# adaLN sums in a 2-layer trunk: a third row-block buffer, low parts in temporaries, sums amid the next pair, small rows through Pool's queue

## The chip, the cores and the metric

One core of a Trainium2 chip runs the whole program. The metric is the device time of one execution in microseconds. Its engines each take their own instructions in program order and wait for one another by semaphores: TensorE (PE) multiplies, VectorE (DVE), ScalarE (ACT) and GpSimd (Pool) work elementwise, and SyncE (SP) issues most of the DMAs; ACT and Pool can issue DMAs too.

## The reference

Two layers of three sublayers each on x of 512 tokens x 1024, all in float32:

```python
c_act = jax.nn.silu(c)
for l in range(DEPTH):
    mod = (c_act @ ada_w[l] + ada_b[l]).reshape(b, N_SUB, 3, 1, D_MODEL)
    h = modulate(x, mod[:, 0, 0], mod[:, 0, 1])
    y = swiglu_ffn(h, ffn1_w_in[l], ffn1_w_out[l])
    x = layer_norm(ALPHA * x + 0.5 * mod[:, 0, 2] * y, ln_g[l, 0], ln_b[l, 0])
    h = modulate(x, mod[:, 1, 0], mod[:, 1, 1])
    proj = h @ mix_w_in[l]
    ...
    x = layer_norm(ALPHA * x + mod[:, 1, 2] * y, ln_g[l, 1], ln_b[l, 1])
    ...
```

The third sublayer is an FFN like the first. The mixer between them is a Mamba-2 scan, an attention and a short convolution side by side. "adaLN" is the first line of the loop: from one vector c come, for each sublayer, a shift, a scale and a gate of 1024 numbers, through a 1024 x 9216 matrix for each layer.

## The kernel before

The sublayers are numbered s = 0 to 5; 1 and 4 are mixers, the others FFNs. A float32 product is made as three matmuls on parts (mm3): each weight block is loaded (ri, or ro for the second matrix; SP), ACT copies its high part (hi, ho) and DVE subtracts it to get the low part (li, lo); the activations are split likewise into hh and hl. So every block costs PE three matmuls for each row of 128, and PE does most of the work.

**An FFN** runs over 11 pairs of column blocks. A pair is two loads (gate and up matrix) of two blocks each, hence four units of 24 matmuls, pf_pair_which_j, in the order 0_0, 1_0, 0_1, 1_1, and then silu (sg), product (af) and split (ah, al). The first pair of an FFN runs in token halves of 256, since the last tile's normalization is still under way. The split weights lie in 6 buffers each, so a block's split waits for the unit six earlier. After pair 5 and after pair 10 out_proj multiplies by the second matrix (po).

**adaLN's matrix product** is not on PE: ada_acc loads eight row blocks (ra, 128x1024, two buffers) and DVE adds each, times a column of silu(c), into two accumulators of 512 (acc, k = 0 to 7; 16 operations). What remains is a sum over the 128 partitions: acc_split makes a high and a low part of each accumulator (gh on ACT, gl on DVE), acc_sum multiplies both by a matrix of ones on PE. For a gate the sum goes through pg into the gate; for shift and scale through pm, then DVE picks the diagonal (dg) and reduces (ada_ss, pieces `which` 1 and 0).

These pieces are Python generators in a list, and tick(), called twice in every pair, advances the first of them by a few steps, so that they are recorded amid an FFN's pairs. A scheduler then orders each engine's instructions by what it reckons; the order is fixed when the program is built. The row blocks of adaLN are named by their first column: gate of s = 0 is acc_2048, then acc_4096 and acc_3072 (scale and shift of the mixer), acc_5120, acc_7168, acc_6144.

**x_affine** multiplies x by the last layer norm's g and adds its b in place (x, after the transposes that feed the next product have read it): 16 Pool operations of 128x512 on four tiles x_102 to x_105. Its vectors lng and lnb are loaded by ln_vectors on ACT's queue. **Pool's rs** is a power of 128x1 in each tile's layer norm. Two sets of small rows (rows_v for vT, rows_ln for lnT), loaded in s = 0, become columns by PE transposes (pv_vT, pv_lnT) after pair 3.

**A mixer** begins with pv (hidden v and the twelve decay inputs of each token), then the B, C and x features (pjm1b, pjm1c, pjm1x: each a product with splits lm.. on DVE). From pv's twelve columns DVE computes a softplus in a chain of tiny operations on 128x48 (v, av, zz, z, ppl, dt, a), and PE sums a over tokens in pcs, which the program places inside pjm1b.

Of the kernel before, what the change touches and what calls it, by code (L numbers as in the profile page):

```python
# [15 lines left out]
P = 128  # L16
# [9 lines left out]
RMS_EPS = 1e-5  # L26
NEG = -1.0e30
NLONG = 28
NTMP = 9
NW = 6  # L30
PAD_W = 16
POS = 1
BPOS = 2
TICK = object()
CR = (2.7, 1.3)
WSZ = 1024

# [32 lines left out]
def trunk(ctx, tc, x, c, ln_in_g, ln_in_b, ada_w, ada_b, ffn1_w_in, ffn1_w_out,  # L70
# [11 lines left out]

    shift("pad0", PAD_W)
    rawp = ctx.enter_context(tc.tile_pool(name="rawp", bufs=2))
    adap = ctx.enter_context(tc.tile_pool(name="adap", bufs=2))
    whp = ctx.enter_context(tc.tile_pool(name="whp", bufs=NW))
    wlp = ctx.enter_context(tc.tile_pool(name="wlp", bufs=NW))
    lp = ctx.enter_context(tc.tile_pool(name="lp", bufs=NLONG))
# [47 lines left out]

    def rows_v(l):
        rows = slot([NROW, P], F32, f"rows{l}")
        act.dma_start(rows[0:72, :], ada_b[l].rearrange("(r p) -> r p", p=P))
        act.dma_start(rows[R_CW:R_CB, :], ssd_conv_w[l].rearrange("k (c p) -> (k c) p", p=P))  # L140
        act.dma_start(rows[R_CB:R_SW, :], ssd_conv_b[l].rearrange("(c p) -> c p", p=P))
        act.dma_start(rows[R_SW:R_NG, :], sconv_w[l].rearrange("k (c p) -> (k c) p", p=P))
        act.dma_start(rows[R_NG:NROW, :], ssd_norm_g[l].rearrange("(c p) -> c p", p=P))
        return rows

    def rows_ln():
        rows = slot([96, P], F32, "rowsl")
        act.dma_start(rows[0:48, :], ln_g.rearrange("l j (r p) -> (l j r) p", p=P))
        act.dma_start(rows[48:96, :], ln_b.rearrange("l j (r p) -> (l j r) p", p=P))
        return rows  # L150

    def rows_first():
# [93 lines left out]
    def acc_split(acc):  # L246

        parts = []
        los = adap.tile([P, 2, 512], F32R, tag="ra", name="gl")
        for h in range(2):  # L250
            hi, lo = tmp([P, 512], "gh", F32R), los[:, h]
            act.activation(hi, acc[h], AF.Copy)
            dve.tensor_tensor(lo, acc[h], hi.bitcast(F32), ALU.subtract)
            parts.append((hi, lo))
        return parts

    def acc_sum(ps, hi, lo):
# [26 lines left out]
    def ada_ss(s):  # L284
        l, j = divmod(s, 3)
        new_mod(s)
        pres = []
        for which in (1, 0):
            acc = None
            for a in ada_acc(l, (j * 3 + which) * D):  # L290
                acc = acc if a is TICK else a
                yield a
            sums = sm.tile([P, KD], F32, tag=f"sums{which}", name=f"sums{which}", bufs=1)
            parts = acc_split(acc)
            yield TICK
# [50 lines left out]
    def ada_gate(s):  # L346
        l, j = divmod(s, 3)
        col = (j * 3 + 2) * D
        gate = [slot([P, 512], F32, f"gate{s}_{h}") for h in range(2)]
        for h in range(2):  # L350
            sp.dma_start(gate[h], ada_b[l, col + h * 512:col + h * 512 + 512].partition_broadcast(P))
        acc = None
        for a in ada_acc(l, col):
            acc = acc if a is TICK else a
            yield a
        parts = acc_split(acc)
        yield TICK
        for h in range(2):
            ps = pb([P, 512], f"pg{s}_{h}")
            acc_sum(ps, *parts[h])  # L360
            dve.tensor_tensor(gate[h], ps, gate[h], ALU.add)
        gates[s] = gate

    def ln_vectors(s):
        g, b = (ln_in_g, ln_in_b) if s == 0 else (ln_g[(s - 1) // 3, (s - 1) % 3], ln_b[(s - 1) // 3, (s - 1) % 3])
        for n, v in (("g", g), ("b", b)):
            for h in range(2):
                a = slot([P, 512], F32, f"ln{n}{s}_{h}")
                act.dma_start(a, v[h * 512:(h + 1) * 512].partition_broadcast(P))
# [6 lines left out]
    def begin(*gens):  # L376
# [2 lines left out]
        credit[0] = 0.0  # L379
        credit[1] = len(pending) and CR[0] if len(gens) > 2 else CR[1]  # L380

    def tick():
        credit[0] += credit[1]
        while pending and credit[0] >= 1:
            try:
                if next(pending[0]) is TICK:
                    break
                credit[0] -= 1
            except StopIteration:
                pending.pop(0)  # L390

# [237 lines left out]
        last[0] = act_last[0]  # L629
        return banks, units[2]  # L630

    def x_affine(s, eng):

        ln_vectors(s)
        for t in range(NT):
            for h in range(2):
                xh = xt[t][:, h * 512:(h + 1) * 512]
                eng.tensor_tensor(xh, xh, aff[s, "g", h], ALU.mult)  # L638
                eng.tensor_tensor(xh, xh, aff[s, "b", h], ALU.add)
# [20 lines left out]
    def ffn(s, w_in, w_out):  # L660
        for gi, grp in enumerate((range(0, 6), range(6, NPAIR))):
            acts = []
            for jp in grp:
# [12 lines left out]
                for i, (ka, kb, a, b, j, which) in enumerate(order):  # L676
                    wh, wl = units[which][j]
                    for k in range(ka, kb):
                        mm3(banks[which][j][:, a:b], wh[:, k, :], wl[:, k, :],
                            hT[0][:, k, a:b], hT[1][:, k, a:b], k == 0, k == KD - 1)  # L680
                    if jp == 0 and i == POS:
                        last_tile[0](mm_last[0])
                for j in range(2):
                    sg = tmp([P, T], "sg")
                    act.activation(sg, banks[0][j], AF.Silu)
                    af = tmp([P, T], "af")
                    dve.tensor_tensor(af, sg, banks[1][j], ALU.mult)
# [22 lines left out]
    def out_proj(s, w_out, r0, acts, half, first, last):  # L710
# [6 lines left out]
        for h in range(2):  # L717
# [482 lines left out]
```

## Time and profile before

| | us |
|---|---|
| three runs | 2003.78, 1996.82, 2000.05 (median 2000.05) |
| the profiled execution | 2000.76 |
| its span, first to last instruction | 1999.0 |
| granted TensorE clock, mean | 0.995 |
| idle of Pool before x_affine, 5 times | 214.7 |

Times in the trace count from the span's start. A row of a timeline gives start, length, engine, line, operation, output and inputs, and in brackets the idle time before it with what ended it. L53 is the line of the helper that records an instruction, so rows are told apart by their tiles. The sublayers begin near 27, 416, 649, 1016, 1396 and 1628 us.

### The profile page before, as it was taken

How to read it: one execution, taken by the hardware profiler on the slowest of the kernel's cores; microseconds unless marked ns; L12 is line 12 of the kernel's file. 1: busy time of each engine (PE TensorE's matmuls, PEld its weight loads, DVE VectorE, ACT ScalarE, POOL GpSimd, SP SyncE). 2: the span in 40 equal slices, each digit the busy share in tenths (PEclk: the TensorE clock that was granted, in tenths of full speed). 3: DMA queues.
4: the chain of work that ended last, by engine and by line, in shares of the span. 5: the costliest groups of instructions: out<-in, count | busy, mean ns of one | idle time of the engine just before them, and what ended most of it. 6: DMA issues, size and time to landing. Idle time of an engine off the chain costs nothing.

```text
span 1999.0 us, 23434 instructions
## 1 busy us (share of the span) xinstructions
PE 1947.5 (97%) x9422; PEld 1627.3 (81%) x9422; DVE 1208.1 (60%) x1770; ACT 690.9 (35%) x1094; POOL 220.6 (11%) x182
## 2 busy tenths in 40 slices
PE   5999999999999999999999999999999999999998
PEld 4777878898878988888898788788978798888887
DVE  8886663477677655543477857435766785433336
ACT  3433223164365432123152322223544553222320
POOL 0230000007100040000005000000260004000000
PEclk9999999999999999999999999999999999999999
DMA  9766542234211544432345746232422144323331
GB/s 327 235 196 225 173 166 82 75 106 127 84 65 53 184 153 163 155 107 93 106 151 188 248 163 229 86 103 57 135 87 83 53 133 142 105 85 106 104 107 43
DMA packets 178605, 263.99 MB, mean 132 GB/s; under 512 B 9676, under 2 KB 124736, under 8 KB 178496
## 3 DMA queue, kind: packets, MB, share of 16 engines
q1 hardware_dynamic: 174000, 254.98, 38.8%
q10 hardware_dynamic: 4496, 7.52, 1.3%
q8 instruction: 74, 1.21, 0.2%
q14 instruction: 35, 0.29, 0.0%
HBM read 260.37 MB, written 2.10 MB: 131 GB/s over the span
## 4 chain that ended last, share of the span: by engine, by line
PE 77%; DVE 11%; DMA 7%; ACT 3%; issue 2%; POOL 0%; POOLq 0%; ACTq 0%; SPq 0%; DVEq 0%
PE pf L53 37%; PE po L53 23%; DMA ra<-in_ada_w_dram 6%; DVE acc L53 4%; PE pz L53 2%; DVE li L53 2%; DVE af L53 1%; PE pjm4x L53 1%; PE pjm1x L53 1%; PE ptr L53 1%; PE pS L53 1%; DMA ri<-in_ffn_w_in_dram 1%; PE py L53 1%; DVE x L53 1%; DVE gy L53 1%
## 5 line engine op out<-in xcount | busy, mean ns | idle before, releaser
L53 PE MATMUL pf<-hh,li 128*128 128x512 f32 (+1 forms) x1504 | 567.8, 378 | 1.4 <-DVE li L53 1.0
L53 PE MATMUL pf<-hl,hi 128*128 128x512 f32 (+1 forms) x1504 | 566.9, 377 | 0.2 <-DVE hl L53 0.2
L53 PE MATMUL pf<-hh,hi 128*128 128x512 f32 (+1 forms) x1504 | 566.9, 377 | 0.0
L53 DVE TENSOR_TENSOR li<-ri,hi 128x1024 fp32r<-128x1024 f32 x176 | 224.7, 1282 | 184.0 <-ACT hi L53 183.8
L53 PEld LDWEIGHTS pf<-hh,li 128*128 128x128 f32 x1504 | 284.4, 189 | 53.4 <-DVE li L53 1.7
L53 PEld LDWEIGHTS pf<-hl,hi 128*128 128x128 f32 x1504 | 284.2, 189 | 52.2 <-DVE hl L53 0.9
L53 PEld LDWEIGHTS pf<-hh,hi 128*128 128x128 f32 x1504 | 284.5, 189 | 51.3
L53 ACT ACTIVATE hi<-ri 128x1024 fp32r<-128x1024 f32 x176 | 185.5, 1060 | 311.1 <-PE pf L53 200.7
L53 PE MATMUL po<-ho,al 128*128 128x512 f32 (+1 forms) x704 | 273.5, 389 | 0.5 <-DVE af L53 0.4
L53 PE MATMUL po<-lo,ah 128*128 128x512 f32 (+1 forms) x704 | 272.9, 388 | 0.0
L53 PE MATMUL po<-ho,ah 128*128 128x512 f32 (+1 forms) x704 | 272.6, 388 | 0.0
L53 DVE TENSOR_TENSOR lo<-ro,ho 128x1024 fp32r<-128x1024 f32 x104 | 127.2, 1223 | 204.5 <-ACT ho L53 204.4
L53 DVE SCALAR_TENSOR_TENSOR acc<-ra,cT,acc 128x512 f32<-128x512 f32 x224 | 172.9, 815 | 67.1 <-DMA ra<-in_ada_w_dram 66.7
L53 ACT ACTIVATE ho<-ro 128x1024 fp32r<-128x1024 f32 x104 | 110.1, 1059 | 286.7 <-PE po L53 160.1
L451 POOL TENSOR_TENSOR rs<-ve,mhalf 128x1 f32<-128x1 f32 x28 | 17.3, 620 | 1277.5 <-DVE ve L53 1276.2
L53 PEld LDWEIGHTS po<-ho,al 128*128 128x128 f32 x704 | 132.2, 188 | 28.2 <-DVE af L53 0.8
L53 PEld LDWEIGHTS po<-ho,ah 128*128 128x128 f32 x704 | 132.2, 188 | 27.0
L53 PEld LDWEIGHTS po<-lo,ah 128*128 128x128 f32 x704 | 132.2, 188 | 26.9
L53 ACT ACTIVATE sg<-pf 128x512 f32<-128x512 f32 x88 | 52.4, 596 | 287.9 <-PE pf L53 270.7
L53 DVE TENSOR_TENSOR af<-sg,pf 128x512 f32<-128x512 f32 x88 | 60.1, 684 | 143.6 <-PE pf L53 141.0
L53 ACT ACTIVATE hf<-ptr,modB,modA 128x128 f32<-128x128 f32 (+1 forms) x168 | 67.0, 491 | 97.6 <-PE ptr L53 84.1
L638 POOL TENSOR_TENSOR x<-x,lng 128x512 f32<-128x512 f32 x48 | 75.5, 1598 | 218.7 <-DMA lng<-in_ln_g_dram 214.7
(397 smaller groups left out, 2488.3 us busy)
## 6 DMA issues: line engine op xcount, KB each, us to landing
ri<-in_ffn_w_in_dram SPq DMA_DIRECT2D x88, 1024.0 KB, 5.1
ra<-in_ada_w_dram SPq DMA_DIRECT2D x128, 512.0 KB, 3.9
ro<-in_ffn_w_out_dram SPq DMA_DIRECT2D x40, 1024.0 KB, 4.9
ro<-in_mix_w_out_dram SPq DMA_DIRECT2D x8, 1024.0 KB, 4.9
rf<-in_ada_w_dram SPq DMA_DIRECT2D x8, 512.0 KB, 8.4
ro<-in_ffn_w_out_dram SPq DMA_DIRECT2D x8, 512.0 KB
rf<-in_ada_w_dram SPq DMA_DIRECT2D x16, 192.0 KB, 6.5
gate<-in_ada_b_dram SPq DMA_DIRECT2D x12, 256.0 KB, 5.5
```

What stands on the lines that cost most here:

```text
L53: ins = f(*a, **k)
L451: pool.tensor_tensor(rs, ve, mhalf[:, 0:1], ALU.pow)
L638: eng.tensor_tensor(xh, xh, aff[s, "g", h], ALU.mult)
```

## The change

- adap, the buffers of row blocks, has 3 instead of 2; the temporaries 7 instead of 9. gl takes two temporaries instead of an adap buffer.
- The sum over partitions follows a new mark, LATE: tick() stops there, and resume(), called after the second of a pair's four units and after the first step of out_proj's first half, records it at that place. acc_sum's first matmul is tied behind the last recorded weight matmul. After the first of two pieces (which = 1) a TICK is added.
- lng, lnb and the small rows are loaded through Pool's queue instead of ACT's.
- x_affine takes a list of tiles, but is called with all four at the same place.

```diff
-NTMP = 9
+NTMP = 7
...
-    adap = ctx.enter_context(tc.tile_pool(name="adap", bufs=2))
+    adap = ctx.enter_context(tc.tile_pool(name="adap", bufs=3))
...
-        act.dma_start(rows[0:72, :], ada_b[l].rearrange("(r p) -> r p", p=P))
+        pool.dma_start(rows[0:72, :], ada_b[l].rearrange("(r p) -> r p", p=P))
...
-        los = adap.tile([P, 2, 512], F32R, tag="ra", name="gl")
         for h in range(2):
-            hi, lo = tmp([P, 512], "gh", F32R), los[:, h]
+            hi, lo = tmp([P, 512], "gh", F32R), tmp([P, 512], "gl", F32R)
...
-        pe.matmul(ps, onesr, hi, start=True, stop=False)
+        after(pe.matmul(ps, onesr, hi, start=True, stop=False), mm_last[0])
...
             parts = acc_split(acc)
-            yield TICK
+            yield LATE
...
             pres.append(sums)
+            if which:
+                yield TICK
...
         parts = acc_split(acc)
         yield TICK
+        yield LATE
...
-                act.dma_start(a, v[h * 512:(h + 1) * 512].partition_broadcast(P))
+                pool.dma_start(a, v[h * 512:(h + 1) * 512].partition_broadcast(P))
...
     def tick():
         credit[0] += credit[1]
+        late[0] = False
         while pending and credit[0] >= 1:
             try:
-                if next(pending[0]) is TICK:
+                got = next(pending[0])
+                late[0] = got is LATE
+                if got is TICK or got is LATE:
                     break
                 credit[0] -= 1
+            except StopIteration:
+                pending.pop(0)
+
+    def resume():
+
+        if late[0]:
+            late[0] = False
+            try:
+                next(pending[0])
             except StopIteration:
                 pending.pop(0)
...
                     if jp == 0 and i == POS:
                         last_tile[0](mm_last[0])
+                    if i == len(order) // 2 - 1:
+                        resume()
...
+                if k == 0 and h == 0:
+                    resume()
```

Where the loads of g and b for s = 1 stood in the program before, on ACT, amid the splits and convolutions (hm1q, cv) of the mixer's C features:

```order
L53 ACTIVATE hm1q_3819<-rm1q 128x1024
L53 ACTIVATE cv_7_3593<-pjm1c_3490,vT_106 128x512
L53 DMA lng_0_3599<-in_ln_g_dram 128x512
L53 ACTIVATE cv_6_3587<-cv_6_3587 128x512
L53 DMA lng_1_3601<-in_ln_g_dram 128x512
L53 DMA lnb_0_3603<-in_ln_b_dram 128x512
L53 DMA lnb_1_3605<-in_ln_b_dram 128x512
```

And in the program of the change on Pool, behind the four rs of the layer norm and the memset of the attention's cf, with the first of x_affine's operations:

```order
L468 TENSOR_TENSOR rs<-ve,mhalf 128x1 x4
L888 MEMSET cf 128x512
L372 DMA lng_0_3605<-in_ln_g_dram 128x512
L372 DMA lng_1_3607<-in_ln_g_dram 128x512
L372 DMA lnb_0_3609<-in_ln_b_dram 128x512
L372 DMA lnb_1_3611<-in_ln_b_dram 128x512
L656 TENSOR_TENSOR x_102<-x_102,lng_0_3605 128x512
L656 TENSOR_TENSOR x_102<-x_102,lng_1_3607 128x512
```

The loads moved from the middle of ACT's features to the first place on Pool after the layer norm; x_affine itself stands behind the same rs and memset in both.

DVE at the start of s = 3 (hl of tile 3, adaLN's acc_2048, the low parts li of pair 1), before:

```order
L53 TENSOR_TENSOR hl_7554<-hf_3_1_8102,hh_7553 128x4x128
L53 SCALAR_TENSOR_TENSOR acc_2048_0_8003<-ra_2048_3_8029,cT,acc_2048_0_8003 128x512
L53 SCALAR_TENSOR_TENSOR acc_2048_1_8004<-ra_2048_3_8029,cT,acc_2048_1_8004 128x512
L53 TENSOR_TENSOR li_1_0_0_8272<-ri_1_0_8269,hi_1_0_0_8271 128x1024
L53 TENSOR_TENSOR li_1_0_1_8276<-ri_1_0_8269,hi_1_0_1_8275 128x1024
L53 SCALAR_TENSOR_TENSOR acc_2048_0_8003<-ra_2048_4_8033,cT,acc_2048_0_8003 128x512
L53 SCALAR_TENSOR_TENSOR acc_2048_1_8004<-ra_2048_4_8033,cT,acc_2048_1_8004 128x512
L53 SCALAR_TENSOR_TENSOR acc_2048_0_8003<-ra_2048_5_8281,cT,acc_2048_0_8003 128x512
L53 SCALAR_TENSOR_TENSOR acc_2048_1_8004<-ra_2048_5_8281,cT,acc_2048_1_8004 128x512
L53 TENSOR_TENSOR li_1_1_0_8296<-ri_1_1_8293,hi_1_1_0_8295 128x1024
```

The same place after the change, from k = 4 on:

```order
L54 SCALAR_TENSOR_TENSOR acc_2048_0_8012<-ra_2048_4_8042,cT,acc_2048_0_8012 128x512
L54 SCALAR_TENSOR_TENSOR acc_2048_1_8013<-ra_2048_4_8042,cT,acc_2048_1_8013 128x512
L54 TENSOR_TENSOR li_1_0_0_8281<-ri_1_0_8278,hi_1_0_0_8280 128x1024
L54 TENSOR_TENSOR li_1_0_1_8285<-ri_1_0_8278,hi_1_0_1_8284 128x1024
L54 SCALAR_TENSOR_TENSOR acc_2048_0_8012<-ra_2048_5_8290,cT,acc_2048_0_8012 128x512
L54 SCALAR_TENSOR_TENSOR acc_2048_1_8013<-ra_2048_5_8290,cT,acc_2048_1_8013 128x512
L54 SCALAR_TENSOR_TENSOR acc_2048_0_8012<-ra_2048_6_8294,cT,acc_2048_0_8012 128x512
L54 SCALAR_TENSOR_TENSOR acc_2048_1_8013<-ra_2048_6_8294,cT,acc_2048_1_8013 128x512
L54 SCALAR_TENSOR_TENSOR acc_2048_0_8012<-ra_2048_7_8298,cT,acc_2048_0_8012 128x512
L54 SCALAR_TENSOR_TENSOR acc_2048_1_8013<-ra_2048_7_8298,cT,acc_2048_1_8013 128x512
L54 TENSOR_TENSOR li_1_1_0_8305<-ri_1_1_8302,hi_1_1_0_8304 128x1024
```

All eight row blocks now stand ahead of li_1_1_0; before, k = 6 and 7 stood behind it. Likewise k = 2 and 3 stand ahead of the two hl of tile 3 where one of them stood before. In s = 2 and s = 5, acc_8192 moves in the same way up to k = 6.

In pair 3 of s = 0 (and of s = 3 alike) DVE takes up acc_4096 only behind pair 2's al_2_1, and k = 5 to 7 stand behind li_4_1_1; before, all of acc_4096 stood ahead of li_4_1_0. After the change (from the last acc of k = 4 on):

```order
L54 SCALAR_TENSOR_TENSOR acc_4096_1_953<-ra_4096_4_970,cT,acc_4096_1_953 128x512
L54 TENSOR_TENSOR li_4_1_1_1189<-ri_4_1_1182,hi_4_1_1_1188 128x1024
L54 SCALAR_TENSOR_TENSOR acc_4096_0_952<-ra_4096_5_974,cT,acc_4096_0_952 128x512
L54 SCALAR_TENSOR_TENSOR acc_4096_1_953<-ra_4096_5_974,cT,acc_4096_1_953 128x512
L54 SCALAR_TENSOR_TENSOR acc_4096_0_952<-ra_4096_6_978,cT,acc_4096_0_952 128x512
L54 SCALAR_TENSOR_TENSOR acc_4096_1_953<-ra_4096_6_978,cT,acc_4096_1_953 128x512
L54 SCALAR_TENSOR_TENSOR acc_4096_0_952<-ra_4096_7_982,cT,acc_4096_0_952 128x512
L54 SCALAR_TENSOR_TENSOR acc_4096_1_953<-ra_4096_7_982,cT,acc_4096_1_953 128x512
L54 TENSOR_TENSOR li_5_0_0_1317<-ri_5_0_1314,hi_5_0_0_1316 128x1024
L54 TENSOR_TENSOR gl<-acc_4096_0_952,gh 128x512
L54 TENSOR_TENSOR gl<-acc_4096_1_953,gh 128x512
```

On PE the sums of these accumulators, pm_1_0 and pm_1_1, stood before pf_4_0_0 and amid its first matmuls; now they stand behind eight matmuls of pf_3_1_1, pair 3's last unit. At the other places the sums move by less: pg from amid pf_2_0_0 to the middle of pair 2, pm_0 of s = 0 and 3 to 10 matmuls into pf_5_0_0 and pf_7_0_0.

More of the change, by code (lines that the diff above doesn't have):

```diff
@@ L34 @@
 TICK = object()
+LATE = object()
 CR = (2.7, 1.3)
@@ L138, in rows_v @@
         rows = slot([NROW, P], F32, f"rows{l}")
-        act.dma_start(rows[0:72, :], ada_b[l].rearrange("(r p) -> r p", p=P))
[L140 to L143, printed above, removed]
+        pool.dma_start(rows[0:72, :], ada_b[l].rearrange("(r p) -> r p", p=P))
+        pool.dma_start(rows[R_CW:R_CB, :], ssd_conv_w[l].rearrange("k (c p) -> (k c) p", p=P))
+        pool.dma_start(rows[R_CB:R_SW, :], ssd_conv_b[l].rearrange("(c p) -> c p", p=P))
+        pool.dma_start(rows[R_SW:R_NG, :], sconv_w[l].rearrange("k (c p) -> (k c) p", p=P))
+        pool.dma_start(rows[R_NG:NROW, :], ssd_norm_g[l].rearrange("(c p) -> c p", p=P))
         return rows
@@ L147, in rows_ln @@
         rows = slot([96, P], F32, "rowsl")
-        act.dma_start(rows[0:48, :], ln_g.rearrange("l j (r p) -> (l j r) p", p=P))
-        act.dma_start(rows[48:96, :], ln_b.rearrange("l j (r p) -> (l j r) p", p=P))
+        pool.dma_start(rows[0:48, :], ln_g.rearrange("l j (r p) -> (l j r) p", p=P))
+        pool.dma_start(rows[48:96, :], ln_b.rearrange("l j (r p) -> (l j r) p", p=P))
         return rows
@@ L380, in begin @@
         credit[1] = len(pending) and CR[0] if len(gens) > 2 else CR[1]
+    late = [False]
     def tick():
         credit[0] += credit[1]
+        late[0] = False
         while pending and credit[0] >= 1:
             try:
-                if next(pending[0]) is TICK:
+                got = next(pending[0])
+                late[0] = got is LATE
+                if got is TICK or got is LATE:
                     break
                 credit[0] -= 1
+            except StopIteration:
[5 more added lines that the diff above has]
+                next(pending[0])
             except StopIteration:
@@ L630, in start, with x_affine @@
         return banks, units[2]
-    def x_affine(s, eng):
-        ln_vectors(s)
-        for t in range(NT):
+    def x_affine(s, eng, tiles=range(NT)):
+        if tiles[0] == 0:
+            ln_vectors(s)
+        for t in tiles:
             for h in range(2):
@@ L694, in ffn @@
                     x_affine(s, pool)
+                if jp == 1:
                     if s == 0:
```

## The prediction

> **What bounds the kernel now.** I read the page first.
>
> ```profile
> PE 1947.5 (97%) x9422; PEld 1627.3 (81%) x9422; DVE 1208.1 (60%) x1770; ACT 690.9 (35%) x1094; POOL 220.6 (11%) x182
> ```
>
> TensorE (PE) is busy 97% of the span and takes its work in program order, so another engine can cost time only where PE's next matmul waits. The chain of waits gives PE's pace: 82.74/364 = 0.227 us for a 512-wide matmul, 5.75/48 = 0.12 for a 256-wide one.
>
> ```profile
> 1255.88 82.74 PE pf L53 x364
> 1016.21 5.75 PE pf L53 x48
> ```
>
> In PE's timeline I looked for gaps beside the adaLN sums (pg, pm), which the change moves, and asked for the windows from the matmul before each gap to the one where the pace is back (start:end, length, busy and count, granted clock, DMA):
>
> ```profile
> 81.93:86.39 4.46, 3.80 (x15) 1.00 0.85 260
> 127.11:136.79 9.68, 6.44 (x17) 0.65 0.61 176
> 157.43:159.68 2.25, 0.72 (x4) 1.00 0.04 15
> 272.41:274.96 2.55, 0.73 (x4) 1.00 0.00 0
> 1130.80:1136.83 6.03, 3.91 (x11) 0.72 0.41 128
> 1249.30:1256.10 6.80, 4.30 (x12) 0.76 0.00 1
> ```
>
> Two matmuls of each count only touch the edges. Length less (count - 2) x 0.227 is the loss: A 1.5, B 6.3, C 1.8, D 2.1, E 4.0, G 4.5, together 20.2 us, 1% of the span: all that the moved sums can win. In B, E and G the granted clock fell to 0.65-0.76, so a wait of 2.5 to 3 us there brought about 2 us of slow matmuls with it.
>
> The wait list then shows what Pool waits for, and its timeline where:
>
> ```profile
> POOL x L638 <- DMA lng<-in_ln_g_dram: 214.7, 5, 46.2
> DVE acc L53 <- DMA ra<-in_ada_w_dram: 68.1, 45, 3.8
> 418.97 0.53 POOL L865 MEMSET cf<- 128x512 f32 x1
> 458.19 2.56 POOL L638 TENSOR_TENSOR x<-x,lng 128x512 f32<-128x512 f32 x2 [38.69 <-DMA lng<-in_ln_g_dram]
> 1019.25 0.86 POOL L451 TENSOR_TENSOR rs<-ve,mhalf 128x1 f32<-128x1 f32 x1 [8.36 <-DVE ve L53]
> 1066.27 5.09 POOL L638 TENSOR_TENSOR x<-x,lng 128x512 f32<-128x512 f32 x4 [46.16 <-DMA lng<-in_ln_g_dram]
> 653.26 0.81 DVE L53 TENSOR_SCALAR x<-x,mv,rs 128x1024 f32<-128x1024 f32 x1 [0.72 <-POOL rs L451]
> ```
>
> x_affine, 16 Pool operations, stands ready some 40 us before it runs in each of sublayers 1 to 5: only lng, issued late in ScalarE's (ACT's) order, holds it. That late issue is a schedule nobody wrote down, and it matters through these rows (acc alone and beside x_affine; a short form alone and beside it; Pool's am and VectorE's xw taking turns; lng's time to land):
>
> ```profile
> 65.70 2.73 DVE L53 SCALAR_TENSOR_TENSOR acc<-ra,cT,acc 128x512 f32<-128x512 f32 x4
> 101.61 6.90 DVE L53 SCALAR_TENSOR_TENSOR acc<-ra,cT,acc 128x512 f32<-128x512 f32 x4
> 654.60 0.88 DVE L53 TENSOR_SCALAR acc<-ra,cT 128x512 f32<-128x512 f32 x2
> 88.33 2.96 DVE L53 TENSOR_SCALAR acc<-ra,cT 128x512 f32<-128x512 f32 x2
> 513.61 1.59 POOL L948 TENSOR_TENSOR am<-a12h,upper 128x512 fp32r<-128x512 f32 x1 [11.12 <-PE pd L53]
> 514.22 1.53 DVE L53 TENSOR_TENSOR xw<-xdt,edec 128x512 f32<-128x512 f32 x1
> lng<-in_ln_g_dram ACTq DMA_DIRECT2D x12, 256.0 KB, 3.6
> ```
>
> One acc takes 0.68 us alone and 1.73 beside x_affine (+1.05); the short form 0.44 and 1.48 (+1.04). The price is the same for both lengths: VectorE (DVE) and Pool alternate, one whole instruction each. So x_affine takes at most 16 x 1.04 = 16.6 us from DVE, wherever it runs. Where DVE has slack, as now, that is free.
>
> **The change, part by part.**
>
> *Pool's queue.* The lng DMAs now follow Pool's last rs. All else that they wait for is over by then. I take x_affine to start 5 us after rs (in a mixer after the memset behind it): 3.6 to land, and about 1.4 for four issues, whose cost on Pool no row shows (bounds: 3.6, and the 38.69 of today). That is 419.5 + 4.5 = 424 in sublayer 1, 1020.1 + 5 = 1025 in 3 and 658 in 2, where x takes up rs at 653.26.
>
> Mixers (1 and 4). What DVE does there now, and PE behind it:
>
> ```profile
> 425.81 0.69 DVE L53 TENSOR_TENSOR hl<-hf,hh 128x512 fp32r<-128x512 f32 x1 [0.36 <-ACT hh L53]
> 427.52 0.69 DVE L53 TENSOR_TENSOR hl<-hf,hh 128x512 fp32r<-128x512 f32 x1 [0.92 <-ACT hh L53]
> 428.28 0.38 PE L53 MATMUL pv<-hm1v,hl 128*128 128x268 f32 x1
> 431.69 0.20 DVE L53 TENSOR_TENSOR v<-v,sgn 128x48 f32<-128x48 f32 x1
> 434.90 1.67 DVE L53 SCALAR_TENSOR_TENSOR ppl<-ppl,z 128x48 f32<-128x48 f32 x7
> 437.08 0.21 DVE L53 TENSOR_TENSOR a<-dt,na 128x48 f32<-128x48 f32 x1
> 438.36 0.30 PE L53 MATMUL pcs<-a,upper 128*128 128x32 f32 x2
> ```
>
> PE's pv starts 0.07 us after the second hl, and pcs 1.07 after a. Walking DVE on from 424 with one Pool operation between two of its own: the split lm1c_0, due at 424.3, ends at 426.4 (behind one Pool operation, and 1.2 long), the two hl at 428.1 and 429.8 instead of 426.5 and 428.2. So hl comes 1.6 us late. Three large splits follow, and from v to a stand 18 tiny operations in series (seven of them in the ppl row), each of which can let one Pool operation in. Of the 16, about 13 fall on busy DVE: 13 x 1.04 = 13.5 us, so a ends near 450.8 instead of 437.3. PE waits 1.6 at pv and, shifted by that, 450.8 - 438.4 - 1.6 = 10.8 at pcs; with the slack rounded, **13 us**. I add 2 for the slow pace after a long wait, as in B, E and G: 15 each, **30** for both. For 128x48 no row shows the price. Its bounds are 0 (only the large operations wait: 4 us a mixer) and 1.04; I take 1.04, since 128x512 and 128x1024 pay the same.
>
> The Trainium skill, "SBUF — State Buffer", "Who interferes with whom", says that the pair of ports that DVE and GpSimd share is an exclusive lock held for the whole instruction, taken by DVE with two SBUF inputs or in its two-port modes. The rows above agree; by that rule only the reciprocal among the 18 would go free, about 1 us less a mixer.
>
> FFNs (2, 3, 5), by sublayer 3:
>
> ```profile
> 1024.85 0.69 DVE L53 TENSOR_TENSOR hl<-hf,hh 128x512 fp32r<-128x512 f32 x1 [1.18 <-ACT hh L53]
> 1027.46 0.69 DVE L53 TENSOR_TENSOR hl<-hf,hh 128x512 fp32r<-128x512 f32 x1
> 1035.39 2.35 DVE L53 TENSOR_TENSOR li<-ri,hi 128x1024 fp32r<-128x1024 f32 x2
> 1022.60 0.36 PE L53 MATMUL pf<-hh,li 128*128 128x256 f32 x1
> ```
>
> From 1022.6 PE has two groups of 24 narrow matmuls before it reads tile 3: 1028.4, the second hl 12 later, 1029.9. Four more groups end at 1039.9, the first wide unit at 1045.4, where li_1_1_0 is needed. Now both are there early (1028.1; 1036.6). After the change k2 and k3 stand ahead of the hls, k4 to k7 ahead of li_1_1_0. From 1025: hl 1026.8, k3 (two acc, 3.5) 1030.3, hl 1032.0: **2.1** late. Then k4 3.5, two li at 2.25 to 1040, six acc 10.4 to 1050.4, li at 1051.9: against 1045.4 + 2.1 that is **4.6** more, and 2 of slow pace: **8.7**. In 2 and 5 PE's needs lie as far from rs, within 0.3 us, but k7 stands behind li_1_1_0: hl 2.4 late, li 1.4: 3.8 each, **7.6**. Sublayer 0 keeps its x_affine at about the same time, behind negm.
>
> *Sums amid the next pair.* Pair 3 of sublayers 0 and 3: pm_1 now stands 8 matmuls into pf_3_1_1, 3 x 5.44 + 1.8 = 18.1 us into the pair, but five acc behind li_4_1_1, whose buffer PE frees at 16.3.
>
> ```profile
> 1039.33 1.06 ACT L53 ACTIVATE hi<-ri 128x1024 fp32r<-128x1024 f32 x1 [3.89 <-DMA ri<-in_ffn_w_in_dram]
> 1251.50 1.24 ACT L53 ACTIVATE gh<-acc 128x512 fp32r<-128x512 f32 x2
> 124.67 1.28 DVE L53 TENSOR_TENSOR gl<-acc,gh 128x512 fp32r<-128x512 f32 x2
> ```
>
> 16.3 + 0.3 + 1.06 (hi) + 1.2 (li) + 5 x 0.68 + 0.6 (gh) = 22.9; li_5_0_0 and two gl, another 2.5, to 25.4. PE fits 1.6 of matmuls in between: 25.4 - 18.1 - 1.6 = 5.7, with slow pace about 8.2. Sublayer 0: 8.2 for A + B = 7.8, **+0.4**; sublayer 3: 8.2 for E, **+4.2**. In sublayer 2 pm_1 moves from behind out_proj's first half to 12 matmuls into it, 2.7 us, while two acc, gh and two gl behind the last split of pair 5 need about 3.8: **+1.1** (bounds 0, and G's 4.5).
>
> *Third buffer, low parts in temporaries.* C, D and G stand behind acc waiting for ra (the 68.1 above); with three in flight I count C at 1.0 (its gl comes later than now), D and G whole (bounds: 0, and all 8.4): 1.0 + 2.1 + 4.5 = **-7.6**. NTMP 7 leaves PE's order in the mixers as it is; I cost it at nothing, hidden behind matmuls there; a tmp that comes late would cost one DVE operation, 0.7.
>
> *Rows.* Sublayer 0's twelve small DMAs now follow x_affine, near 115. At 1 us each, an estimate, they land near 130, as PE leaves pair 3's stall. Nothing.
>
> Sum: 30 + 8.7 + 7.6 + 0.4 + 4.2 + 1.1 - 7.6 = +44.4, on the profiled 2000.76 (0.7 above the median of the three): **2045**.
>
> **The rivals.**
> - *Tiny operations hardly wait* (lower bound above): mixers 4 each, 8 instead of 30: 2023. For it: no row of that size beside Pool. Against it: the fixed +1.04.
> - *Not slower: x_affine still starts late.* If issue and landing on Pool's queue take over 17.6 us from the memset's end (419.5 to 437.1), it starts behind a, and behind li_1_1_0 too; then 30 + 8.7 + 7.6 = 46.3 drop out, leaving 2000.8 - 1.9 = 1999, or 1986 if pair 3 doesn't stall (-8.2 and E's 4.2). For it: no Pool DMA in this trace. Against: 3.6 us to land elsewhere.
> - *Pool's DMAs are starved by DVE.* Where each issue takes 3 us, 12 rows end near 115 + 37 and PE waits at pv from 131: +21; the FFN terms (16.3) fall away since x_affine starts 14 us after rs, the mixers' stay: 2050. The Trainium skill's same page, the "DVE blocks DMA" note, tells of it: descriptors that GpSimd can't write while DVE holds the ports, 3.1 us for 0.62. No row here shows it.
>
> **How the numbers follow.** Forecast 0.54 (2030 to 2058: mixers 10 to 17 each, FFNs 8 to 20), tiny operations free 0.18 (2012 to 2030), late start 0.18 (1986 to 2007), starved 0.10 (2040 to 2060). Leaving out the late start, the range is 2012 to 2060. About 0.3%, 6 us, can be told from no change: faster 0.07 and same 0.11, both from the late start; slower 0.82.
>
> **What would show it.** Right: Pool's x near 424, 658, 1025, 1403 and 1637; ppl at over 1 us each; PE waiting over 8 us at pcs for DVE a; a PE wait at li in pair 1 of sublayer 3; pm_1 waiting for gh in pair 3. Wrong: ppl at 0.24 beside Pool; x_affine 15 us or more behind rs; PE waiting at pv_vT for rows; or pair 3 running through.

## The result, and the profile after

The changed kernel takes **2057.84 us** (median of four runs, 2052.34 to 2062.66), the kernel before 1999.34 (four runs): ratio 1.0289, 95% interval 1.0256 to 1.0323. The profiled run took 2059.78, its span 2058.1; the mean granted clock fell from 0.995 to 0.985.

The page's line of engines and the wait list (waits in us: total, times, longest), after:

```profile
PE 1963.0 (95%) x9422; PEld 1639.8 (80%) x9422; DVE 1236.9 (60%) x1770; ACT 691.5 (34%) x1094; POOL 243.0 (12%) x222
PE pcs L54 <- DVE a L54: 20.8, 2, 10.4
PE pf L54 <- DVE hl L54: 15.5, 4, 5.4
PE pf L54 <- DVE af L54: 7.0, 3, 2.5
POOL x L656 <- DMA lng<-in_ln_g_dram: 9.1, 5, 2.2
```

Pool's wait for lng is down from 214.7 to 9.1, and three PE waits have come that before didn't have (but 0.2 for hl): for a in the mixers, for hl and af in the FFNs, 43 us together. DVE has more busy time than before with the same 1770 instructions (1236.9 against 1208.1): it takes turns with Pool.

A sublayer's length, from the start of its fourth rs on Pool to that of the next sublayer's, says where the 59 us lie (computed from the rows of rs; one profiled execution each; the last three kernels are experiments below):

| s | before | after | difference | LN rows on ACT | x_affine held | no transfers, 5 us behind rs |
|---|---|---|---|---|---|---|
| 0 (FFN) | 393.8 | 393.0 | -0.9 | 390.7 | 391.4 | 392.4 |
| 1 (mixer) | 234.2 | 249.3 | +15.1 | 234.2 | 234.5 | 249.7 |
| 2 (FFN) | 366.6 | 376.3 | +9.7 | 366.4 | 366.4 | 376.6 |
| 3 (FFN) | 378.3 | 385.4 | +7.0 | 373.6 | 378.4 | 383.3 |
| 4 (mixer) | 234.2 | 250.5 | +16.3 | 234.4 | 235.7 | 249.9 |
| 5 (FFN) | 360.9 | 372.2 | +11.2 | 361.0 | 360.9 | 371.3 |

**Mixer.** Pool's timeline at s = 1, after:

```profile
418.00 0.55 POOL L468 TENSOR_TENSOR rs<-ve,mhalf 128x1 f32<-128x1 f32 x1 [7.21 <-DVE ve L54]
418.49 0.53 POOL L888 MEMSET cf<- 128x512 f32 x1
418.96 1.26 POOL L372 DMA_DIRECT2D lng<-in_ln_g_dram  x2
420.21 1.06 POOL L372 DMA_DIRECT2D lnb<-in_ln_b_dram  x2
423.31 3.58 POOL L656 TENSOR_TENSOR x<-x,lng 128x512 f32<-128x512 f32 x2 [2.03 <-DMA lng<-in_ln_g_dram]
```

Four issues cost Pool 2.3 us, and x_affine starts 5.3 behind rs. DVE and PE meanwhile, after (the same ppl row took 1.67 before, v 0.20, and a started at 437.08):

```profile
433.55 1.30 DVE L54 TENSOR_TENSOR v<-v,sgn 128x48 f32<-128x48 f32 x1
438.30 1.27 DVE L54 TENSOR_SCALAR v<-v 128x48 f32<-128x48 f32 x1
439.70 0.45 DVE L54 RECIPROCAL av<-av 128x48 f32<-128x48 f32 x1
440.89 1.19 DVE L54 TENSOR_TENSOR z<-zz 128x48 f32<-128x48 f32 x1
443.31 5.72 DVE L54 SCALAR_TENSOR_TENSOR ppl<-ppl,z 128x48 f32<-128x48 f32 x7
449.55 0.21 DVE L54 TENSOR_TENSOR a<-dt,na 128x48 f32<-128x48 f32 x1
449.90 0.60 PE L54 MATMUL pcs<-a,upper 128*128 128x32 f32 x2 [10.44 <-DVE a L54]
```

An operation on 48 columns that takes 0.2 us alone takes 1.2 to 1.3 beside a Pool operation. The reciprocal keeps its 0.45; the last of the chain are short again, since x_affine is over at 448.2.

**FFN.** Pool, DVE and PE in s = 2, after (the first two rows: Pool's issues of lng and what DVE does beside them), and the window behind PE's first wait (start:end, length, then busy and count for PE, PEld, DVE, ACT, POOL; granted clock; DMA share; GB/s):

```profile
667.82 1.54 POOL L372 DMA_DIRECT2D lng<-in_ln_g_dram  x2
667.89 0.81 DVE L54 TENSOR_SCALAR x<-x,mv,rs 128x1024 f32<-128x1024 f32 x1 [0.73 <-POOL rs L468]
677.92 2.58 DVE L54 SCALAR_TENSOR_TENSOR acc<-ra,cT,acc 128x512 f32<-128x512 f32 x2 [4.54 <-DMA ra<-in_ada_w_dram]
680.43 1.74 DVE L54 TENSOR_TENSOR hl<-hf,hh 128x512 fp32r<-128x512 f32 x1
682.09 4.53 DVE L54 TENSOR_TENSOR li<-ri,hi 128x1024 fp32r<-128x1024 f32 x2
686.54 10.28 DVE L54 SCALAR_TENSOR_TENSOR acc<-ra,cT,acc 128x512 f32<-128x512 f32 x6
696.74 4.54 DVE L54 TENSOR_TENSOR li<-ri,hi 128x1024 fp32r<-128x1024 f32 x2
701.20 0.74 DVE L54 SCALAR_TENSOR_TENSOR acc<-ra,cT,acc 128x512 f32<-128x512 f32 x1
701.87 0.67 DVE L54 TENSOR_TENSOR af<-sg,pf 128x512 f32<-128x512 f32 x1
682.22 0.58 PE L54 MATMUL pf<-hl,hi 128*128 128x256 f32 x1 [4.59 <-DVE hl L54]
682.61 0.42 PE L54 MATMUL pf<-hh,hi 128*128 128x256 f32 x1
687.73 0.40 PE L54 MATMUL pf<-hh,hi 128*128 128x256 f32 x1
702.60 0.50 PE L54 MATMUL pf<-hh,li 128*128 128x512 f32 x1 [2.17 <-DVE af L54]
682.00:687.00 5.00, 4.78 (x22) 4.78 (x23) 5.00 (x4) 1.55 (x2) 5.00 (x3) 0.50 0.24 91
```

hl stands behind the two acc of k = 3, and these wait 4.54 us for their row block. From hl on, every DVE operation is about 1.04 longer, until x_affine ends at 700.2. PE's narrow matmuls behind the wait start 0.213 us apart (24 steps between the two rows at 682.61 and 687.73) instead of 0.12, at half the clock: 2.2 us more. Then PE runs into a second wait, which ends with af. 4.59 + 2.2 + 2.17 = 9.0 of this sublayer's 9.7 us.

### The profile page after: what moved, and what is told of

Same layout as the page of the kernel before. It is cut to its first block, busy times and chain, and to the rows that moved or that the text cites. A ratio compares the mean times of both kernels' runs of the same rounds, so it can differ in the third digit from the quotient of the medians.

```text
span 2058.1 us, 23453 instructions
## 1 busy us (share of the span) xinstructions
PE 1963.0 (95%) x9422; PEld 1639.8 (80%) x9422; DVE 1236.9 (60%) x1770; ACT 691.5 (34%) x1094; POOL 243.0 (12%) x222
## 4 chain that ended last, share of the span: by engine, by line
PE 80%; DVE 10%; DMA 5%; issue 2%; ACT 2%; POOL 1%; POOLq 0%; DVEq 0%; SPq 0%; ACTq 0%
PE pf L54 41%; PE po L54 23%; DMA ra<-in_ada_w_dram 4%; DVE acc L54 3%; PE pz L54 2%; DVE li L54 2%; PE pjm4x L54 1%; PE pjm1x L54 1%; PE pS L54 1%; DVE ppl L54 1%; PE py L54 1%; DVE af L54 1%; DVE hl L54 1%; DVE x L54 1%; PE pjm1c L54 1%
## 5 line engine op out<-in xcount | busy, mean ns | idle before, releaser
L54 PE MATMUL pf<-hl,hi 128*128 128x512 f32 (+1 forms) x1504 | 570.9, 380 | 15.5 <-DVE hl L54 15.5
L54 DVE SCALAR_TENSOR_TENSOR acc<-ra,cT,acc 128x512 f32<-128x512 f32 x224 | 184.6, 875 | 41.0 <-DMA ra<-in_ada_w_dram 41.0
L657 POOL TENSOR_TENSOR x<-x,lnb 128x512 f32<-128x512 f32 x48 | 80.1, 1690 | 0.4
```

The source lines that it names most:

```text
L54: ins = f(*a, **k)
```

## The experiments

Each ran with the kernel before on the same chip; ratios are to that, with 95% intervals.

### x_affine held back

```diff
+        held = None
+        if s > 0:
+            scr = sm.tile([P, 1], F32, tag="held", name="held", bufs=2)
+            held = eng.tensor_tensor(scr, late_src, mhalf[:, 0:1], ALU.mult)
...
-                eng.tensor_tensor(xh, xh, aff[s, "g", h], ALU.mult)
+                after(eng.tensor_tensor(xh, xh, aff[s, "g", h], ALU.mult), held)
...
-                    x_affine(s, pool)
+                    x_affine(s, pool, late_src=ah[:, 0:1].bitcast(F32))
...
-        x_affine(s, pool)
+        x_affine(s, pool, late_src=xbc[7][:, 0:1])
```

> The changed kernel, with one tiny Pool operation added ahead of x_affine in sublayers 1 to 5, which reads a value that is late (the last of pair 1's ah in an FFN, the last C feature in a mixer). PE, DVE, ACT and SP have the same order as in the changed kernel, and lng is still loaded early through Pool's queue; only x_affine starts some 40 us later, about where it started before the change. Theory T (x_affine takes turns with DVE, and it matters where): the waits at pcs (10.5 us) and pv go in both mixers, -31; in the FFNs the wait for af in pair 1 goes (2.4 each) and the wait for hl shrinks from 5 to 6 us to about 3, since acc k3 ahead of it still waits for its row block: about 2008, between 2000 and 2016. Rival Q (loads through Pool's queue themselves, or their taking ACT's loads away): no change, 2050 to 2062. Rival O (the new order of DVE with the third buffer and the late sums): no change, 2050 to 2062.

2000.01 us, 1.0013 (1.0003 to 1.0023). One tiny Pool operation ahead of x_affine, and all else of the change as it was: all but 2 to 3 of the 59 us are gone, with a's wait, hl's and af's. So they come from where x_affine lies, in the FFNs with its transfers. What is left is the other parts of the change, and here they bring nothing. Two waits of pair 3 that the prediction had are seen here, timeline of PE in s = 0 and s = 3:

```profile
126.22 0.80 PE L54 MATMUL pm<-gh,onesr 128*128 128x512 f32 x1 [5.11 <-ACT gh L54]
1105.75 0.80 PE L54 MATMUL pm<-gh,onesr 128*128 128x512 f32 x1 [5.34 <-ACT gh L54]
```

With the slow matmuls behind them PE loses 8.0 and 8.3 us there. In the mixers the transfers stayed where the change put them, and only the arithmetic moved. In the FFNs this kernel held the transfers of lng and lnb as well (`held` stands ahead of them on Pool); three kernels below take the two apart.

### The LayerNorm rows alone on ACT's queue again

```diff
-                pool.dma_start(a, v[h * 512:(h + 1) * 512].partition_broadcast(P))
+                act.dma_start(a, v[h * 512:(h + 1) * 512].partition_broadcast(P))
```

> The changed kernel with lng and lnb loaded through ACT's queue again, the small rows still through Pool's. PE and SP keep the order of the changed kernel, DVE but for 8 rows in the mixers. T: as the held x_affine, within 5 us of it, about 2008. Q: here the loss goes, and in the held one it does not. O: no change, 2050 to 2062.

1995.75, 0.9990 (0.9980 to 0.9999). One line of the diff carries the slowdown; the third buffer, the low parts, the late sums and the small rows on Pool together gain about 2 us.

### The LayerNorm rows on Pool's queue, in the kernel before

The same line the other way, and nothing else of the change:

> The kernel before with nothing changed but lng and lnb through Pool's queue. T: x_affine starts some 5 us behind the layer norm as in the changed kernel; the mixers lose 13 to 16 us each; in the FFNs hl stands ahead of k3 and li_1_1_0 ahead of k6, so they lose only 1 to 3 each: about 2035, between 2028 and 2045. Q: 2040 to 2058 as well. O: 1997 to 2003.

2048.96, 1.0262 (1.0242 to 1.0283). The price is there without the rest: PE waits 20.9 for a, 15.2 for hl. That is 14 more than expected; the FFNs lost 11.9, 4.8 and 8.0 (s = 2, 3, 5; by the rows of rs). As expected hl stands ahead of k = 3 there, but behind the acc of k = 2, and in s = 2 these wait 3.61 us for their row block, where before they waited 0.69: the late block needs neither the third buffer nor the new order.

### Pool busy beside the chain, with memsets

x_affine and its transfers are held back as in the first experiment, and Pool writes zeros during the chain:

```diff
-            pool.memset(cf, 0.0)
+            for _ in range(40):
+                pool.memset(cf, 0.0)
```

> The held kernel with 40 memsets of 128x512 in place of one on Pool in each mixer, right behind the layer norm, some 21 us of Pool that writes and reads nothing, beside DVE's tiny operations. If only a Pool operation that reads takes turns with DVE (T, and the rule of the Trainium skill, SBUF - State Buffer, Who interferes with whom): the tiny operations stay at 0.2 us and the time within 5 us of the held kernel. Rival M (any Pool operation takes turns): each of the 18 waits up to 0.5 us, a is late by about 8 us, both mixers together 14 us above the held kernel.

2002.37, 1.0017 (1.0002 to 1.0033), as with x_affine held. Timeline of Pool and DVE, s = 1:

```profile
417.95 23.77 POOL L893 MEMSET cf<- 128x512 f32 x40
430.62 0.20 DVE L54 TENSOR_TENSOR v<-v,sgn 128x48 f32<-128x48 f32 x1
432.42 0.59 DVE L54 TENSOR_SCALAR av<-ee 128x48 f32<-128x48 f32 x1
434.24 1.66 DVE L54 SCALAR_TENSOR_TENSOR ppl<-ppl,z 128x48 f32<-128x48 f32 x7
436.67 0.43 DVE L54 CAST a12h<-a 128x48 fp32r<-128x48 f32 x1
```

Pool is busy without a break, and ppl runs at its old pace. It is not Pool's being busy that DVE pays for, but operations on Pool that also read, as x_affine's do. Of the chain, only two operations with one input are longer, av by 0.41 (0.18 before) and the cast by 0.24 (0.19).

### Transfers early, arithmetic late

As the first experiment, but with the four transfers ahead of `held` in Pool's order, also in the FFNs:

```diff
+            after(held, aff_dma[0])
```

> After with its LayerNorm-row transfers where the change put them (right behind rs, on Pool's queue), and only x_affine's 16 additions and products held back: behind ah in the FFNs, behind cv in the mixers. The first held kernel (2000.0) had moved the transfers of the FFNs as well, so it doesn't say whether hl is late there by turns with Pool or by the 1 MB of lng and lnb that lands ahead of the ada_w block that acc k3 needs. Theory of turns: no hl wait in sublayers 2, 3 and 5, 2000 (1998 to 2003). Theory of transfers: the ra block still lands about 4 us late and PE waits 3.5 to 5 for hl in each of the three, 2012 (2007 to 2017). Both at once would show as about 1 us or 2 of wait, 2004.

2006.59, 1.0031 (1.0015 to 1.0046), some 4 to 7 us more than with the transfers late. DVE and PE at the place of the first wait in s = 2 (in the last row, DVE at the same place in the first experiment):

```profile
663.87 1.41 DVE L54 SCALAR_TENSOR_TENSOR acc<-ra,cT,acc 128x512 f32<-128x512 f32 x2 [4.73 <-DMA ra<-in_ada_w_dram]
665.20 0.68 DVE L54 TENSOR_TENSOR hl<-hf,hh 128x512 fp32r<-128x512 f32 x1
665.94 0.58 PE L54 MATMUL pf<-hl,hi 128*128 128x256 f32 x1 [2.53 <-DVE hl L54]
657.04 1.42 DVE L54 SCALAR_TENSOR_TENSOR acc<-ra,cT,acc 128x512 f32<-128x512 f32 x2 [0.52 <-DMA ra<-in_ada_w_dram]
```

The 1 MB of lng and lnb (four loads of 256 KB) that is now issued just ahead of the row block makes DVE wait 4.73 us for it, against 0.52 with the transfers held; PE waits 2.5 for hl in each of the three FFNs (7.7 in all, 0.2 before). That lies between the theories' numbers, and under the range of the theory of transfers (2007 to 2017).

### No transfers, x_affine at once

This kernel leaves out the real rows of g and b in s = 1 to 5: x_affine takes the identity in their place.

```diff
-        if tiles[0] == 0:
+        if tiles[0] == 0 and s == 0:
             ln_vectors(s)
...
+                if s:
+                    xh = xh.rearrange("p (a b) -> p a b", b=P)
+                    row = ident[:, None, :].to_broadcast([P, 4, P])
-                eng.tensor_tensor(xh, xh, aff[s, "g", h], ALU.mult)
-                eng.tensor_tensor(xh, xh, aff[s, "b", h], ALU.add)
+                eng.tensor_tensor(xh, xh, row if s else aff[s, "g", h], ALU.mult)
+                eng.tensor_tensor(xh, xh, row if s else aff[s, "b", h], ALU.add)
```

> After without the LayerNorm-row transfers of sublayers 1 to 5: x_affine multiplies by, and adds, the identity instead (it leaves out the affine step's real rows), with the same 16 operations of the same size, from right behind rs. Theory of transfers: ra lands in time; hl is late by turns alone, at most 2.1 in each FFN instead of 5.0 to 5.9; with the af waits of pair 1 the FFNs lose about 10 instead of 28, the mixers 10 to 16 each: 2040 (2030 to 2046). Theory of turns: hl still stalls 5 in each FFN and the sum stays at 2050 to 2058.

2043.38, 1.0217 (1.0203 to 1.0231). The number fits the theory of transfers, but the experiment doesn't tell: with nothing to wait for, x_affine followed each row block's own rs, before the fourth one, and the waits moved to other places (PE waited up to 4.7 us for x at the transposes). It is no test of what happens 5 us later.

### No transfers, x_affine 5 us behind rs

As the last kernel, the real rows left out, with a delay on Pool ahead of x_affine:

```diff
+            held = eng.tensor_tensor(scr, xt[3][:, 0:1], mhalf[:, 0:1], ALU.mult)
+            fill = sm.tile([P, 4, P], F32, tag="fill", name="fill", bufs=1)
+            for _ in range(6):
+                nxt = eng.memset(fill, 0.0)
+                after(nxt, held)
+                held = nxt
```

> As the kernel without transfers (the identity in place of the LayerNorm rows), but x_affine waits for the last row block's x and then for six memsets of 128x512 on Pool (0.59 us each by the memset kernel): it starts 4 to 5 us after the last rs, as in after, and no transfer goes with it. By turns alone: hl late by 2.1 to 2.4 in sublayers 2, 3 and 5 where after has 5.0 to 5.9, af waits of pair 1 as in after (2.4 each with the slow pace), mixers as in after (12 to 13 stalled, 15 to 16 with the slow pace): about 2047 (2042 to 2052). If the 5 us come from turns alone: 2054 to 2060. If they come from transfers alone, no hl wait: 2040.

2056.59, 1.0280 (1.0265 to 1.0296), the same as after. Waits, and the second wait of s = 2 on DVE and PE:

```profile
PE pf L54 <- DVE af L54: 18.7, 3, 7.4
PE pf L54 <- DVE hl L54: 4.7, 4, 1.6
683.06 10.30 DVE L54 SCALAR_TENSOR_TENSOR acc<-ra,cT,acc 128x512 f32<-128x512 f32 x6
693.28 4.51 DVE L54 TENSOR_TENSOR li<-ri,hi 128x1024 fp32r<-128x1024 f32 x2
697.71 1.75 DVE L54 SCALAR_TENSOR_TENSOR acc<-ra,cT,acc 128x512 f32<-128x512 f32 x1
699.38 0.67 DVE L54 TENSOR_TENSOR af<-sg,pf 128x512 f32<-128x512 f32 x1
700.10 0.79 PE L54 MATMUL pf<-hh,li 128*128 128x512 f32 x1 [5.69 <-DVE af L54]
```

Without the transfers hl is only 1.6 us late, as by turns alone; but af is then 5.7 late and more. The two waits add up to 23.4 us here and to 22.5 in after. So in the FFNs the transfers set where PE waits first, and the turns set how much it loses in all. I read it so: a wait for hl gives Pool time to get on, and is paid back at af. The next kernel fits that, but no run here tests it alone.

### Half of x_affine early

The transfers and row blocks 0 and 1 stay where the change put them, blocks 2 and 3 are held:

```diff
         for t in tiles:
+            if s > 0 and t == 2:
+                scr = sm.tile([P, 1], F32, tag="held", name="held", bufs=2)
+                held = eng.tensor_tensor(scr, late_src, mhalf[:, 0:1], ALU.mult)
+                after(held, last)
```

> After with x_affine's first eight operations (row blocks 0 and 1) where the change put them and the other eight held back as in the held kernels. The price is paid once for each Pool operation that falls between two of VectorE before a: eight end near 437, the tiny operations behind run at their old length, and a comes about 3 us after PE asks for it instead of 10.5: mixers 5 each instead of 15; FFNs keep the 5 of hl, and lose less at af: 2034 (2028 to 2040). If instead the tiny operations are slow for another reason than x_affine's operations beside them (their start behind the late splits, a longer latency), pcs stalls 8 or more still: 2050.

2031.60, 1.0154 (1.0131 to 1.0176), as the theory of turns had it. Timeline in s = 1:

```profile
434.68 2.28 POOL L664 TENSOR_TENSOR x<-x,lnb 128x512 f32<-128x512 f32 x1
435.72 1.29 DVE L54 TENSOR_SCALAR v<-v 128x48 f32<-128x48 f32 x1
438.33 1.66 DVE L54 SCALAR_TENSOR_TENSOR ppl<-ppl,z 128x48 f32<-128x48 f32 x7
440.52 0.21 DVE L54 TENSOR_TENSOR a<-dt,na 128x48 f32<-128x48 f32 x1
440.87 0.59 PE L54 MATMUL pcs<-a,upper 128*128 128x32 f32 x2 [2.90 <-DVE a L54]
```

Of Pool's operations the eighth ends at 436.96, and from there on DVE's tiny operations have their old lengths. PE waits 2.9 instead of 10.4. The FFNs keep their wait for hl (15.5 in all, as after) and have none for af.

### The second wait: af or li_1_1_0

```diff
-        return [split(v[:, :, j * P:(j + 1) * P], f"{name}_{j}", prev) for j in range(2)]
+        return [split(v[:, :, j * P:(j + 1) * P], f"{name}_{j}", second if j and second else prev) for j in range(2)]
...
-ln_done[0] if s > 0 and jp == 1 else None))
+ln_done[0] if s > 0 and jp == 1 else None,
+                                       first_af[0] if s > 0 and (jp, which) == (1, 1) else None))
...
-                    dve.tensor_tensor(af, sg, banks[1][j], ALU.mult)
+                    mul = dve.tensor_tensor(af, sg, banks[1][j], ALU.mult)
+                    if (jp, j) == (0, 0):
+                        first_af[0] = mul
```

> After with one edit: in sublayers 1 to 5 of the FFN kind the split li_1_1_1, which PE needs two units later, stands behind the first af of pair 0 on VectorE instead of ahead of it. If PE's wait in pair 1 is for the accumulator bank that this af frees (and not for li_1_1_0, which stands at its old place), the wait shrinks by what one li takes less what slips ahead of af: in sublayers 2 and 5 by 2.27 - 0.74 = 1.5, to 0.8 and 0.9, in sublayer 3 by 1.2, to 1.5, and with waits that short the slow matmuls behind them go too (1.4 to 1.7 each in 3 and 5): about 7 in all, 2050 (2046 to 2055). If it is for li_1_1_0 the three waits stay at 2.3 to 2.7 and the time at 2057.

2054.15, 1.0269 (1.0252 to 1.0287); the interval overlaps that of after, so a gain of 7 isn't shown. The trace of s = 2 settles the question all the same:

```profile
697.54 2.32 DVE L54 TENSOR_TENSOR li<-ri,hi 128x1024 fp32r<-128x1024 f32 x1
699.78 2.42 DVE L54 SCALAR_TENSOR_TENSOR acc<-ra,cT,acc 128x512 f32<-128x512 f32 x2
702.12 0.67 DVE L54 TENSOR_TENSOR af<-sg,pf 128x512 f32<-128x512 f32 x1
702.85 0.50 PE L54 MATMUL pf<-hh,li 128*128 128x512 f32 x1 [2.72 <-DVE af L54]
```

li_1_1_0 (the row at 697.54) is done at 699.86; PE goes on at 702.85, 0.06 behind the end of af. The program has four of these accumulator banks, pair 0 holds all, and pf_1_1_0 takes the one that af reads. The size was off since a second acc slipped ahead of af; the three waits came to 5.4 instead of 7.0.

### The other parts alone

The third buffer and the low parts in temporaries in the kernel before:

> Before with the third row-block buffer and the low parts in temporaries alone (sums and rows as before). By the prediction's terms C 1.0, D 2.1 and G 4.5 go and A, B, E stay: 7.6 under the before of the same chip, 1990 (1988 to 1993). Rival: what D and G lost comes back as a wait of the same sums for gy or gh a few us later, as the held kernel showed 1.0 at each of two places: 3 to 5 under it, 1993 to 1996. Nothing gained would mean that the two waits of the one profile are not in most executions.

2000.73, 1.0011 (1.0000 to 1.0022): nothing gained. In its profile C, D, E and G are gone, but PE loses more at pg of s = 0 (2.9 and 4.0 us with the slow matmuls, where A had 1.5) and 3.5 at pg of s = 3, and the second pm_1 of s = 0 (acc_7168), behind the out_proj after pair 5, loses some 4.3, with a wait of 2.56 for gy.

Then the LayerNorm rows on ACT and pm_1 back at a pair's start, and the same with the transposes of the small rows one pair later:

```diff
-            yield LATE
+            yield TICK if which else LATE
...
-                if s == 0 and jp == 3:
+                if s == 0 and jp == 4:
```

> After with the LayerNorm rows on ACT's queue again (as the second kernel, 1995.75) and pm_1 back at a pair's start (the other sums amid the next pair). By the prediction pm_1's stall in pair 3 of sublayers 0 and 3 (7.3 and 2.5 in the second kernel's profile) goes, and B and E of before come back in its place if the third buffer doesn't remove them: pm_1's wait there then is 6.3 and 4.0 again, 1996. If with three buffers the accumulator is ready at pair 4, both are gone: 1987 (1985 to 1991).

> The kernel with LayerNorm rows on ACT and pm_1 at the pair's start (1996.4), and with the transposes of sublayer 0's small rows one pair later, so that the copies vT no longer stand ahead of gl on VectorE. If pm_1's 6.5 there is the copies', it falls to 2 to 3 and the time to 1993 (1990 to 1995), 0.3% under before. If gh and gl aren't ready by then in any case, or the copies hold up pm_0 a pair later, 1996.

The first took 1996.38, 0.9979 (0.9970 to 0.9988): the third buffer makes E's sum ready at the pair's start, but in s = 0 pm_1 still loses 8.1 us in three waits (1.75 for gh, 1.24 for gl, 2.41 for vT), 4.9 of them from the wait for vT on; the 6.5 of the second expectation is without the first wait. The second took **1993.06, 0.9962 (0.9948 to 0.9976)**, the lowest of all and faster than both kernels, though its interval overlaps that of the first: with the copies vT out of its way, pm_1 loses 3.1 us, in two waits:

```profile
127.99 0.51 PE L54 MATMUL pm<-gh,onesr 128*128 128x512 f32 x1 [1.15 <-ACT gh L54]
129.73 0.50 PE L54 MATMUL pm<-gl,onesr 128*128 128x512 f32 x1 [1.23 <-DVE gl L54]
```

## Why the prediction was right, and where a size was off

2045 was forecast, 2057.8 came: slower, as forecast, by the mechanism forecast, but only 0.2 inside the upper end of the range (2030 to 2058). By sublayer (terms of the sum against the table's column of differences): s = 0 -2.7 against -0.9; s = 1 15 against 15.1; s = 2 4.9 against 9.7; s = 3 8.4 against 7.0; s = 4 15 against 16.3; s = 5 3.8 against 11.2.

- **Start of x_affine.** Right: 5.3, 4.9, 4.9, 5.5 and 4.6 us behind rs in sublayers 1 to 5. Issuing took 0.54 to 1.02 each, not 0.35, and nothing hung on that.
- **Mixers.** Right in place, mechanism and size: pv 1.6 and 1.7 late (1.6 forecast), pcs 10.4 (10.8), and what is left of the 15.1 of s = 1, for slow matmuls, is 3.1 (2 forecast). The open price of a 128x48 operation is settled at the upper bound, about 1.0 us more: half of x_affine's operations gives 2.9 of wait, none of them gives none. The Trainium skill ("SBUF — State Buffer", "Who interferes with whom") says that a DVE instruction with two SBUF inputs collides with a GpSimd instruction that reads SBUF and not with one that only writes it: the memsets agree (ppl 1.66). It also has an instruction with at most one SBUF input, outside the two-port modes, go free: the reciprocal agrees, at 0.45 beside x_affine as alone.
- **FFNs, the step that failed.** Here the prediction put li_1_1_0 as the last thing PE waits for (4.6 late in s = 3, 1.4 in s = 2 and s = 5). I stopped walking DVE's queue one stop too early: PE asks at the same moment for the accumulator bank that af frees, and af stands behind li_1_1_1 too, and in s = 2 and s = 5 behind an acc of k = 7. By turns that is 2.3, or 2.3 + 1.7 us, more than li_1_1_0. Without transfers the three waits for af were 18.7 us in all, with slow matmuls behind them, where the terms for li came to 7.4. Forecast for the three sublayers 16.3, and 8 to 20 as its range; after less the kernel with LayerNorm rows on ACT gives 9.9 + 11.8 + 11.2 = 32.9. With this part so far outside its own range, that the total stayed inside is luck: pair 3 of s = 3, below, erred the other way.
- **hl.** 2.1 to 2.4 forecast, 1.6 by turns alone, some 5 in after. That 1 MB of lng lands ahead of the row block that acc of k = 3 needs was not in the sum. It moves the wait forward and adds little: without transfers, the three FFNs are 2.7 us shorter in all (by the table).
- **Pair 3.** The 8.2 are there in s = 0 and s = 3 with x_affine held (8.0, 8.3). In after they are 6.6 and 1.6, in the kernel with rows on ACT 7.3 and 2.5: in s = 3 the later accumulator isn't always late. This is why s = 3 came out smaller than its sum.
- **Third buffer.** -7.6 forecast, nothing measured alone. C, D and G go, but pm_1 behind the out_proj after pair 5, where PE before waited 0.3 for gy, loses 0.7 to 4.3 there in s = 0 (nothing in the last kernel) and 1.0 to 3.8 in s = 3, and pg loses more where it isn't put later. The +1.1 in s = 2 is not seen in any run.
- **Rows of s = 0 through Pool.** Nothing, as forecast: each of the twelve took 0.50 to 0.59 to issue, not 1, and PE doesn't wait at pv_vT. Where pm_1 waited for vT (before, 3.24), it was for the copies and not for the loads.
- **The rivals.** The tiny operations do wait. x_affine doesn't start late by itself; made to, it gives 2000.0, where the rival had 1999. Starvation at 3 us an issue isn't seen: Pool issued at 0.50 to 0.62 us each beside DVE's two-input operations. But the first issue of each FFN took 1.00 to 1.02, beside DVE's x of 0.81 us, which has one tensor input (the rows of s = 2 above, at 667.8; the second issue of the row took 0.54). The note "DVE blocks DMA" of the Trainium skill ("SBUF — State Buffer") ties the stall to DVE operations in a two-port mode, and the same page of the Trainium skill has 3.1 us for a load beside a copy, which no run here shows.
- **Other terms.** The parts of the change other than lng, -1.9 by the sum, came out near that (2 us faster with the rows on ACT) through errors that cancel: less from the buffer, less lost in s = 2 and s = 3. Two slips in the working change little: 1051.9 against 1045.4 + 2.1 is 4.4, not 4.6; and the late start's 1986 takes off E's new 4.2 but leaves in E's own 4.0, without which it is 1982.

The 20 us that the sums could have won were thus given back in three places: pair 3 (a sum that is put earlier asks earlier), gy behind out_proj, and vT ahead of pm_1. The last kernel but one got 3 us of it, the last 7.

## What to carry to other kernels

A load that comes late can be what keeps an off-path engine's work out of the way of another engine; before it is hurried, ask which queue its consumer will share, and with what, at the new time. Where two engines take turns by whole instructions, count instructions, not bytes: a chain of tiny operations pays the most. And when an engine falls behind, walk its queue to the last instruction that the bound engine asks for, buffers it must free among them, not to the first.

## What the runs showed of the hardware

- Beside Pool operations that read and write SBUF, most DVE operations on SBUF are 1.0 to 1.1 us longer whatever their length (0.20 to 1.30 at 128x48, 1.2 to 2.3 at 128x1024). Shorter ones were a reciprocal (0.45, as alone) and a subtraction with an input in PSUM, TensorE's result memory (vl, 0.41; 0.42 before). Beside memsets on Pool those with two inputs are unchanged; a one-input TENSOR_SCALAR and a CAST were 0.41 and 0.24 longer there, which I had not expected.
- A DMA issue on Pool's queue took 0.50 to 0.62 us beside two-input DVE operations and 1.00 to 1.02 beside a one-input one of 0.81 us, lng landed 4.3 us after the first issue began, and 1 MB issued ahead of a 512 KB block made that block 4.2 us later (4.73 of wait against 0.52).
- A PE wait of 4.59 us was followed by 5 us at half the clock (0.50 in the window); waits for af of 2.27 and 2.72 us were followed by some 1.7 us of slow matmuls too, one of 2.17 was not. No length divides them: a wait of 1.75 for hl (half of x_affine early, s = 4) was followed by three at 0.50, one of 3.18 for gl (third buffer alone, s = 3) by none.
